# One layer of a gated hybrid block: the second block of x loaded through ScalarE's queue

## The chip, the core and the metric

The kernel runs on one core of a Trainium2 chip. A core has a matrix engine (TensorE, PE in the profile), whose weight loads are listed apart (PEld), and three engines for everything else: VectorE (DVE), ScalarE (ACT) and GpSimd (POOL). SyncE (SP) only issues transfers. ScalarE and GpSimd can issue transfers too. Each issuing engine has a queue of its own; the transfers themselves are carried by the core's 16 DMA engines.

The metric is the device time of one execution in microseconds, the median of several runs.

## What is computed

One layer over a sequence of 512 positions and 1024 channels, all in float32:

```python
h = rms_norm(x, norm_mix_g)
cb, cc, cin, q, k, v, f_logit, g_logit = split(h @ w_in)
y_conv = (cb * causal_dwconv(cc * cin, conv_mix_w)) @ w_out_conv
o = forgetting_attention(q, k, v, log_sigmoid(f_logit + b_f))    # 8 heads of 64, causal
g_conv, g_attn = split(sigmoid(g_logit + b_gate))
x = x + (g_conv * y_conv + g_attn * (o @ w_out_attn)) @ w_o
h = rms_norm(x, norm_ffn_g)
a, b = split(causal_dwconv(h @ w_up, conv_ffn_w))                # 2 x 2816
x = x + (silu(a) * b) @ w_down
out = rms_norm(x, norm_f_g)
```

Only the beginning matters here: the first part of `h @ w_in`, the columns for v and for the forget logits.

## The kernel before

**Layout and precision.** x comes transposed as `xT`, 128 partitions x 8 blocks x 512 positions: block kb holds channels 128 kb to 128 kb + 127. A product in float32 is made of three faster ones: each operand is split into a high part in the reduced type fp32r and a low part, the remainder, and TensorE adds high x high, low x high and high x low in PSUM. For a weight, the high part is a copy (`wh`) and the low part a subtraction (`wl`); for x, the copy is scaled by the norm's gain from the small table `vec` (`xgh`), and the low part is one multiply-and-subtract (`xgl`). The division by the root mean square is put on later, when results leave PSUM.

**Start.** The first work of TensorE is a loop over the eight blocks kb (lines 452 to 500). For each, 24 matmuls multiply x's block with the weight block `v{kb}` (128 x 520 values): 4 tiles of 128 positions, two column groups (`pa` of 264 columns, `pb` of 256), three products each. All eight blocks add up in the same banks of PSUM. Ahead of the loop nine warm-up matmuls on a tile of ones keep TensorE busy (line 115). Block 0 is taken in smaller pieces: its x comes in two halves, and its weights in two parts, which ScalarE's queue (line 179) and SyncE's queue (line 180) issue.

**The preparation of a block.** For blocks 0 and 1, VectorE makes `wh` (lines 271 and 273); from block 2 on, ScalarE (line 275). VectorE makes all `wl` (line 279) and `xgl` (line 467). ScalarE makes `xgh` (line 458), then squares of x for the norm. In block 1 `xgh` is written ahead of the weight's split.

**Loading.** The weights of the whole kernel are one list, `stream`; `load` issues its next entries, at first a few blocks ahead, later as buffers come free. x is loaded by `load_x`. The order at the start is this:

```python
load_x(0, halves[0])
load(0)
load_x(0, halves[1])
for kb in range(1, AHEAD + 1):      # AHEAD = 3
    load_x(kb)
    load(kb)
for kb in range(AHEAD + 1, KB):
    load_x(kb)
```

All of `load_x` and all of `load` but the first part of weight block 0 goes through SyncE's queue. `vec` goes through GpSimd's (line 99). On ScalarE a small activation (line 110) stands ahead of line 179; it makes the engine load its function table.

**What sets the order.** Instructions passed to `keep` stay in program order on their engine. These are all matmuls, all transfers of `load` and `load_x`, and the preparation of the eight v blocks. The others are placed by the framework's planner, which also sets which instruction waits for which semaphore; a small list `later` with due positions and time allowances, written by hand, decides where in the program much of the later work is put. Transfers of SyncE and ScalarE take their completion semaphores in turn from a small set, so a transfer can be held until an earlier one has landed.

**After the start.** The projections for attention and convolution (`p_in`, `p_q`, `p_k`), attention, gates, `w_o`, and the channel mixer (`p_up`, `dn`) follow, all driven by the same weight stream. Part of the large products uses seven block products in place of eight; the sums of weight blocks that this needs are formed by adding transfers on GpSimd's queue (line 211). These stages are not touched by the change.

Of the kernel before, what the change touches and what calls it, by code (L numbers as in the profile page):

```python
# [70 lines left out]
def block_kernel(ctx, tc, xT, vecs, wv, win, wmix, wo, wup, wst, wdp, outT):  # L71
# [3 lines left out]
    nc = tc.nc  # L75
# [6 lines left out]
    def keep(ins):  # L82
        return tc.keep_in_program_order(ins)
# [334 lines left out]
    xs = []  # L418

    def load_x(kb, cs=slice(0, S)):  # L420
        if kb == len(xs):
            if kb % 2 == 0:
                if kb == 4:
                    ap.tile([P, S], F32, tag="pp", name="pp_", bufs=NPP)
                    ap.tile([P, 4], F32, tag="m", name="m_", bufs=6)
                load_x.t = ap.tile([P, 2, S], F32, tag="qt" if kb < 4 else "ka", name=f"xs{kb}", bufs=2)
            xs.append(load_x.t[:, kb % 2, :])
        keep(nc.sync.dma_start(xs[kb][:, cs], xT[:, kb, cs]))


    halves = [slice(0, S // 2), slice(S // 2, S)]
# [3 lines that stand above are left out]
    for kb in range(1, AHEAD + 1):  # L435
        load_x(kb)
        load(kb)
# [1100 lines left out]
```

## Time and profile before

| | |
|---|---|
| median of 3 runs | 693.18 us (693.14 to 693.18) |
| the profiled execution | 693.12 us |
| its span in the profile | 691.3 us |
| TensorE busy | 681.8 us, 99% of the span |
| VectorE, ScalarE, GpSimd busy | 80%, 53%, 28% |
| bytes moved by transfers | 137.54 MB |

The span goes from the first to the last instruction of the program; the time of the execution holds 1.8 us more. In the rows of the profile, L428 is line 428 of the kernel. "PEq", "SPq" and so on are the sequencers, which issue and wait. A row of the time line gives start and duration in us, engine, line, operation, what it writes and reads, its shape, how many were merged into it, and in brackets how long the engine had been idle and what ended that. A row of the waits gives who waited for whom, the total in us, how often, and the longest. `raw_v` is the landing place of the v weight blocks, `xs` that of x's blocks.

### The profile page before, as it was taken

To read this page: it belongs to the slowest core of one execution; us is meant where nothing else is said; L and a number is where in the kernel's file an instruction comes from. 1 tells how busy PE (TensorE), PEld (TensorE's weight loads), DVE (VectorE), ACT (ScalarE), POOL (GpSimd) and SP (SyncE) were. 2 spreads that over 40 slices of the span, in tenths; PEclk is the share of its full clock that TensorE was granted. 3 is DMA by queue.
4 is the path that set the end of the run, shared out by engine and by line. 5 is a ranking of instruction groups with operands and counts; after the bars stand their busy time and mean duration, and the time that the engine had idled before them with its cause. 6 is when DMAs were issued, how large, how long until landed. Compare 5 with 4: busy or idle time off the path is not lost.

```text
span 691.3 us, 14713 instructions
## 1 busy us (share of the span) xinstructions
PE 681.8 (99%) x5936; PEld 679.9 (98%) x5936; DVE 555.2 (80%) x861; ACT 367.9 (53%) x581; POOL 192.7 (28%) x203
## 2 busy tenths in 40 slices
PE   8999999999999999999999999999999999999996
PEld 8999999999999999999999999999999999999995
DVE  5777887967578778868879699998787898988894
ACT  5675755555555444446564455546444545445672
POOL 6124947542020201214400144340100314332000
PEclk9999999999999999999999999999999999999998
DMA  8628999562577686788997498888945986876513
GB/s 291 240 62 287 217 246 208 129 134 92 167 162 210 166 261 198 239 310 210 161 315 230 129 251 216 184 233 253 250 148 187 288 256 162 191 167 161 192 31 123
DMA packets 66165, 137.54 MB, mean 199 GB/s; under 512 B 5888, under 2 KB 31760, under 8 KB 65840
## 3 DMA queue, kind: packets, MB, share of 16 engines
q1 hardware_dynamic: 45384, 107.28, 46.9%
q0 software_dynamic: 18896, 26.03, 24.4%
q10 hardware_dynamic: 1816, 3.29, 1.3%
q8 instruction: 46, 0.75, 0.4%
q14 instruction: 23, 0.19, 0.1%
HBM read 132.31 MB, written 47.71 MB: 260 GB/s over the span
## 4 chain that ended last, share of the span: by engine, by line
PE 94%; DVE 3%; DMA 1%; ACT 0%; issue 0%; SPq 0%; DVEq 0%; ACTq 0%
PE dn L327 28%; PE p_up L309 18%; PE p_in L309 14%; PE p_wo L309 6%; PE p_up L327 5%; PE yc L309 3%; PE ya L309 3%; PE p_q L309 2%; PE p_k L309 2%; PE o L658 2%; PE pa L477 2%; PE pb L479 1%; PE tp L641 1%; PE pdB L309 1%; PE pdA L309 1%; DVE wl_up L279 1%
## 5 line engine op out<-in xcount | busy, mean ns | idle before, releaser
L211 POOL DMA_DIRECT2D f<-in_wst_dram x69 | 80.0, 1367 | 26.7 <-DMA f<-f 26.3
L309 PE MATMUL p_up<-x1h,wh_up 128*128 128x256 f32 x416 | 81.1, 276 | 0.0
L309 PE MATMUL p_up<-x1h,wl_up 128*128 128x256 f32 x416 | 81.0, 276 | 0.0
L309 PE MATMUL p_up<-x1l,wh_up 128*128 128x256 f32 x416 | 81.0, 276 | 0.0
L279 DVE TENSOR_TENSOR wl_F<-raw_F,wh_F 128x1024 fp32r<-128x1024 f32 (+1 forms) x43 | 56.1, 1304 | 19.0 <-ACT wh_F L275 18.9
L275 ACT ACTIVATE wh_F<-raw_F 128x1024 fp32r<-128x1024 f32 (+1 forms) x43 | 44.5, 1035 | 40.8 <-PE dn L327 26.4
L309 PEld LDWEIGHTS p_up<-x1h,wh_up 128*128 128x128 f32 x416 | 62.7, 188 | 0.0
L309 PEld LDWEIGHTS p_up<-x1l,wh_up 128*128 128x128 f32 x416 | 62.6, 188 | 0.0
L309 PEld LDWEIGHTS p_up<-x1h,wl_up 128*128 128x128 f32 x416 | 62.6, 188 | 0.0
L1234 POOL TENSOR_TENSOR ge<-fu,fu 128x512 f32<-128x512 f32 x11 | 23.2, 2108 | 123.3 <-DVE fu L570 92.6
L309 PE MATMUL p_in<-xgh,wh_in 128*128 128x256 f32 x288 | 56.8, 279 | 0.0
L309 PE MATMUL p_in<-xgh,wl_in 128*128 128x256 f32 x288 | 56.6, 278 | 0.0
L309 PE MATMUL p_in<-xgl,wh_in 128*128 128x256 f32 x288 | 56.5, 278 | 0.0
L275 ACT ACTIVATE wh_P<-raw_P 128x768 fp32r<-128x768 f32 (+1 forms) x43 | 35.2, 820 | 34.5 <-PE dn L327 23.1
L279 DVE TENSOR_TENSOR wl_P<-raw_P,wh_P 128x768 fp32r<-128x768 f32 (+1 forms) x43 | 41.7, 970 | 14.6 <-ACT wh_P L275 8.6
L279 DVE TENSOR_TENSOR wl_up<-raw_up,wh_up 128x1024 fp32r<-128x1024 f32 x34 | 45.2, 1328 | 7.5 <-ACT wh_up L275 7.4
L327 PE MATMUL dn<-gh,wh_F 128*128 128x256 f32 x216 | 51.0, 276 | 0.0
L327 PE MATMUL dn<-gl,wh_F 128*128 128x256 f32 x216 | 51.0, 276 | 0.0
L275 ACT ACTIVATE wh_up<-raw_up 128x1024 fp32r<-128x1024 f32 x34 | 35.8, 1054 | 20.4 <-PE p_up L309 9.8
L309 PEld LDWEIGHTS p_in<-xgh,wh_in 128*128 128x128 f32 x288 | 44.7, 188 | 0.7
L309 PEld LDWEIGHTS p_in<-xgl,wh_in 128*128 128x128 f32 x288 | 43.7, 188 | 0.0
L309 PEld LDWEIGHTS p_in<-xgh,wl_in 128*128 128x128 f32 x288 | 43.6, 188 | 0.0
(343 smaller groups left out, 2208.5 us busy)
## 6 DMA issues: line engine op xcount, KB each, us to landing
raw_F<-f SPq DMA_DIRECT2D x40, 512.0 KB, 5.8
raw_up<-in_wup_dram SPq DMA_DIRECT2D x34, 512.0 KB, 5.6
raw_P<-in_wst_dram SPq DMA_DIRECT2D x40, 384.0 KB, 5.9
raw_in<-in_win_dram SPq DMA_DIRECT2D x24, 512.0 KB, 4.1
f<-in_wst_dram POOLq DMA_DIRECT2D x41, 256.0 KB, 7.7
f<-in_wst_dram SPq DMA_DIRECT2D x19, 512.0 KB, 7.1
f<-in_wst_dram POOLq DMA_DIRECT2D x19, 512.0 KB, 8.4
f<-f SPq DMA_DIRECT2D x38, 256.0 KB, 6.0
```

The source lines that it names most:

```text
L211: return lambda: keep(nc.gpsimd.dma_start(dst, src, accum_op=ALU.add))
L275: ins = nc.scalar.activation(hi, raw, AF.Copy)
L279: ins = nc.vector.tensor_sub(lo, raw, hi.bitcast(F32))
L309: keep(nc.tensor.matmul(out[:, cs], w, x[:, cs], start=start and i == 0 and c == 0, stop=stop and i == 2 and c == len(cut) - 1,))
L327: keep(nc.tensor.matmul(out, wl if x == 1 else wh, xl if x == 2 else xh, start=opens and bk not in seen, stop=closes and bk not in left,))
L477: keep(nc.tensor.matmul(pa[t][:, :VW], xt, w[:, VB:], start=start, stop=stop))
L479: keep(nc.tensor.matmul(pb[t], xt, w[:, :VB], start=start and t % 2 == 0, stop=stop and t % 2 == 1))
L641: keep(nc.tensor.transpose(tp[:, ks], pt[:, ks], ident))
L658: keep(nc.tensor.matmul(o[:, 2 * P * e + c0 : 2 * P * (e + 1)], w, x[:, kb, c0:], start=e == 0 and kb == 0 and i == 0, stop=e == 1 and kb ...
L1234: keep(nc.gpsimd.tensor_mul(ge, a.rearrange(halves_of, h=2), b.rearrange(halves_of, h=2)))
```

## The change

The transfer of block 1 of x is issued by ScalarE in place of SyncE. All other blocks stay with SyncE, and the place of the call in the program stays the same.

```diff
@@ -425,7 +425,7 @@
                     ap.tile([P, 4], F32, tag="m", name="m_", bufs=6)
                 load_x.t = ap.tile([P, 2, S], F32, tag="qt" if kb < 4 else "ka", name=f"xs{kb}", bufs=2)
             xs.append(load_x.t[:, kb % 2, :])
-        keep(nc.sync.dma_start(xs[kb][:, cs], xT[:, kb, cs]))
+        keep((nc.scalar if kb == 1 else nc.sync).dma_start(xs[kb][:, cs], xT[:, kb, cs]))
```

## The prediction, made before the result was known

> **What bounds the kernel now.** I read the page first, then the waits of TensorE, then the busy time by stage. From the page:
>
> ```profile
> span 691.3 us, 14713 instructions
> ...
> PE 94%; DVE 3%; DMA 1%; ACT 0%; issue 0%; SPq 0%; DVEq 0%; ACTq 0%
> ```
>
> The chain that ended last is matmuls for 94% of the span; transfers are 1% of it. The waits of TensorE, all that there are, and the busy time by stage (columns of the second: stage, its length, busy us of each engine, granted clock, DMA share, GB/s) say where the other part lies:
>
> ```profile
> PE warm L115 <- DVE ones L107: 1.1, 1, 1.1
> PE pa L477 <- DVE wh_v L273: 0.8, 1, 0.8
> PE p_up L327 <- DVE wl_up L279: 0.7, 1, 0.7
> ...
> 0.00:8.80 8.80, 6.79 (x42) 6.43 (x43) 3.41 (x8) 3.64 (x6) 7.29 (x21) 1.00 0.71 218
> 8.80:30.00 21.20, 21.20 (x178) 21.20 (x179) 15.07 (x23) 12.12 (x20) 5.37 (x9) 1.00 0.87 313
> 30.00:660.00 630.00, 629.22 (x5506) 628.00 (x5506) 515.44 (x792) 338.63 (x530) 180.00 (x175) 1.00 0.75 201
> ```
>
> From 8.80 us on TensorE has no idle time until 30, and 0.78 us in the 630 us after that. So whatever moves the matmul at 8.80 moves the end by as much, if the rest is left in its order; and TensorE's whole idle time from its first real matmul to 660 us is 0.8 + 0.7 us. That caps a gain at the start at 0.84 us, the idle time just before 8.80. The chain of waits over the first 60 us says what ends that idle time:
>
> ```profile
> 1.65 0.43 SPq L428
> 2.12 0.43 SPq L428
> 2.60 5.46 DMA raw_v<-in_wv_dram
> 8.09 0.58 DVE wh_v L273
> ...
> 8.80 0.36 PE pa L477
> ```
>
> It runs back from the matmul to VectorE's copy of weight block 1 (v1 below), to the 5.46 us from that transfer's issue to its landing, and then to SyncE's own issue instructions. The issue at 2.12 is the one that the change takes away from SyncE: the second block of x (x1). It stands on the chain, directly ahead of v1.
>
> **The change part by part.** It removes one issue from SyncE's queue, adds one to ScalarE's, and puts x1's 256 KB behind ScalarE's own first transfer in place of behind x0's second half. The queues of SyncE and ScalarE, in order of time (start, us, what):
>
> ```profile
> 1.19 0.42 SPq L180 DMA_DIRECT2D raw_v<-in_wv_dram  x1
> 1.65 0.91 SPq L428 DMA_DIRECT2D xs<-in_xT_dram  x2
> 2.60 0.43 SPq L182 DMA_DIRECT2D raw_v<-in_wv_dram  x1
> 4.97 3.71 SPq L428 DMA_DIRECT2D xs<-in_xT_dram  x4
> ...
> 0.74 1.28 ACT L110 ACT_TABLE_LOAD   x1 [0.74 <-PEq L1524]
> 1.04 0.44 ACTq L179 DMA_DIRECT2D raw_v<-in_wv_dram  x1
> 4.28 0.91 ACT L458 ACTIVATE xgh<-xs,vec 128x256 fp32r<-128x256 f32 x2 [2.04 <-DMA vec<-in_vecs_dram]
> 7.41 0.72 ACT L458 ACTIVATE xgh<-xs,vec 128x512 fp32r<-128x512 f32 x1 [2.22 <-DMA xs<-in_xT_dram]
> 10.06 0.71 ACT L458 ACTIVATE xgh<-xs,vec 128x512 fp32r<-128x512 f32 x1
> ```
>
> *SyncE, removed.* One issue and the step to the next: 2.60 - 2.12 = 0.48 us. v1 is issued at 2.12 instead of 2.60, and each later one up to the first held one 0.48 us earlier. The hold is inside the 3.71 us of four issues near 5 us, which wait for earlier landings. Those are blocks 4 to 7; the DMA queue is full then and TensorE has no gap, so an earlier or later release there costs nothing.
>
> *ScalarE, added.* One issue of 0.44 us (the price of its row at 1.04), right behind that row: about 1.5 to 1.95. It is covered: ScalarE does nothing after its table work until 4.28, 2.04 us idle, waiting for the small table vec. Without that cover it would cost 0.44. SyncE's 0.42 at 1.19 overlaps ScalarE's 0.44 at 1.04, and neither is longer than the others, so two queues issuing side by side cost nothing extra here. x1 itself is issued about 0.6 us earlier than at 2.12.
>
> *When v1 lands.* The last landing in the chain is v1's, at 2.60 + 5.46 = 8.06. If its time in flight stays 5.46, it lands 0.48 earlier: copy at 7.61, matmul at 8.32. That is the first term: 0.48 us. It is bounded below by nothing gained, since the same engines must move the same bytes ahead of v1 (x0, v0, x1). It is bounded above by the other thing that the matmul group needs, its predecessor.
>
> *The group before.* The 24 matmuls of block 0:
>
> ```profile
> 4.84 0.51 PE L477 MATMUL pa<-wh_v,xgh 128*128 128x264 f32 x2
> ...
> 7.57 0.39 PE L479 MATMUL pb<-wh_v,xgl 128*128 128x256 f32 x2
> ```
>
> They end at 7.96, so the idle time is 8.80 - 7.96 = 0.84, and restart cannot be earlier than 7.96. This group may itself come later: x1 now runs beside v0 and x0's second half instead of behind them. What x1 can take from them depends on the rate (by stage, the busy time of the instructions on x alone, then granted clock, DMA share, GB/s):
>
> ```profile
> 2.00:4.00 2.00, 0.00 (x0) 0.00 (x0) 1.00 0.97 275
> 4.00:6.00 2.00, 0.65 (x2) 0.91 (x2) 1.00 0.69 166
> 6.00:8.00 2.00, 0.22 (x1) 0.59 (x1) 1.00 0.98 349
> 10.00:24.00 14.00, 3.79 (x6) 7.24 (x13) 1.00 1.02 372
> ```
>
> At 372 GB/s, 262,144 bytes are 0.70 us. So block 0 ends between 7.96 (x1 stays behind) and 8.66 (all of x1 goes ahead of what block 0 needs). With half of x1 ahead, the middle, it is 8.31: no later than v1's own 8.32. I take restart at 8.33, a gain of 0.47, with 0 and 0.84 as ends.
>
> *What is late next.* Block 2's group starts 24 matmuls after 8.80, about 11.65, and at 11.18 in the forecast. Its x is ready at 10.06 + 0.71 = 10.77 even if it does not move at all. So block 2 does not give the gain back, and its weights were issued earlier too.
>
> **The sum.** Span 691.3 - 0.47 = 690.83. The profiled execution took 693.12, 1.82 more than its span and 0.06 less than the median of 693.18; 690.83 + 1.82 + 0.06 = 692.71, taken as 692.7, 0.07% under the time before. That is less than the 0.2% (1.39 us) which a measurement of this kernel can tell from no change. The likeliest case's own range is 692.3 (the whole 0.84) to 693.2.
>
> **The rivals.**
>
> *Hidden: the engines share.* x1 takes its turn beside v0 and x0, so block 0 ends later by what v1 gains. Speaking for it: DMA share is 0.97 from 2 to 4 us, when x1 would start. Against it: from 4 to 6 us the share is 0.69 at 166 GB/s, so there is room that x1 and v1 could use. With all 0.70 us ahead of block 0 the restart is at 8.66, a gain of 0.14: 693.0; if v1 also lands as before, 693.2. [...]
>
> *Slower: x1's slow start stands ahead of block 0.* One row speaks for it: x1 landed only at 7.41, while x0's second half was in use by 4.28 + 0.91 - 0.49 = 4.70, with the shortest of these activations here:
>
> ```profile
> L458 ACT ACTIVATE xgh<-xs,vec x9: 493/709/724, 4.3 to 24.0; 128x512 fp32r<-128x512 f32 x7, 128x256 fp32r<-128x256 f32 x2
> ```
>
> So 256 KB took up to 2.71 us, where 0.70 would do: the 166 GB/s stretch. If that slowness belongs to x1's reads and now holds the engines while v0, vec and x0's second half are queued, block 0 ends at 7.96 + 2.71 = 10.67, 1.87 us after 8.80: 695.05. It decides from a delay of block 0 over 0.84 us on; over 2.23 us it is slower by more than 0.2%. Against it: x0 and v0 are issued earlier than x1 on both queues.
>
> *The planner orders the rest anew.* Only what stands under `keep` has a written order; the others are placed by the framework's planner, which sees another start. What one such order costs, from the 0.7 us wait above (ScalarE's row, then VectorE's):
>
> ```profile
> 605.68 1.05 ACT L275 ACTIVATE wh_up<-raw_up 128x1024 fp32r<-128x1024 f32 x1
> ...
> 606.22 1.80 DVE L1261 TENSOR_TENSOR gl<-go,gh 128x512 fp32r<-128x512 f32 x2
> 607.95 0.74 DVE L567 SCALAR_TENSOR_TENSOR fu<-fz,vec,fu 128x511 f32<-128x511 f32 x1
> 608.61 1.21 DVE L279 TENSOR_TENSOR wl_up<-raw_up,wh_up 128x1024 fp32r<-128x1024 f32 x1
> ```
>
> wh_up is done at 606.73, but wl_up stands behind three others and starts at 608.61, and TensorE idles 0.73. Two more such places give 694.2 beside the forecast's gain, four 695.6, and four without that gain 696.1. One fewer gives at best 693.18 - 0.84 - 0.73 = 691.6. There is little left to win by order and much to lose. Against it: past block 0 all work hangs on TensorE's pace, so a shift alike for all engines leaves the order as it is.
>
> **How the numbers follow.** Forecast (restart between 7.96 and 8.70, order kept) 0.43. Hidden (693.0 to 693.2) 0.20. Slow start ahead of block 0 0.12, of which 0.07 over 0.2%. New order 0.25: 0.20 over 0.2% slower, 0.03 faster by more, 0.02 within. Faster: 0.04 and 0.01 for a gain that adds up from both, 0.05; slower 0.07 + 0.20 = 0.27; within 0.2%: 0.68. The range goes from 692.3 (whole idle time gone) to 696.1 (four such waits more); it leaves out about 0.06 below and 0.12 above.
>
> **What would show it.** Right: x1's issue on ScalarE's queue near 1.5; v1's issue at about 2.1; VectorE's copy of v1 near 7.6; block 1's first matmul near 8.33; and TensorE's waits after that the same two in number, the late one about 0.47 us earlier. Hidden: the first matmuls of block 0 after 4.84 stretched, block 1 at 8.66 or later. Slow start: waits of ScalarE or VectorE for x or weights inside block 0. New order: a longer list of TensorE's waits past 30 us. The prediction is wrong if block 1 starts after 8.80, or if new waits past 30 us add up to more than 0.5 us.

## The result and the profile after

The changed kernel is slower: 695.80 us median of 7 runs (693.86 to 696.64) against 693.14 for the kernel before (692.77 to 693.41). The ratio, estimated from all these runs, is 1.0033, with a 95% interval from 1.0023 to 1.0043. The forecast was 692.7. The profiled execution took 694.50 us, one of the quicker ones of the changed kernel; its span is 692.7.

The page, and the waits of TensorE, of the changed kernel:

```profile
span 692.7 us, 14713 instructions
...
PE 94%; DVE 3%; DMA 1%; ACT 0%; issue 0%; DVEq 0%; ACTq 0%; POOLq 0%
```

```profile
PE pa L477 <- ACT xgh L458: 1.4, 1, 1.4
PE warm L115 <- DVE ones L107: 1.1, 1, 1.1
PE p_up L327 <- DVE wl_up L279: 0.7, 1, 0.7
```

The list is as short as before, and the late wait is the same, so nothing past the start was ordered anew. The wait for VectorE's copy of weight block 1 is gone, since block 0 now ends later than that copy. A wait for `xgh`, the scaled copy of x's block 0, stands in its place, and it is longer: 1.4 us where 0.8 was. The chain of waits over the first 12 us says why (start, us, what):

```profile
1.28 4.77 DMA vec<-in_vecs_dram
6.07 0.52 ACT xgh L458
6.63 0.51 PE pa L477 x2
```

The chain no longer runs through v1 but through `vec`, the table of 20 KB that GpSimd's queue brings. It is issued at 1.28 as before, but takes 4.77 us where ScalarE's wait for it ended at 4.28 before. ScalarE's and SyncE's queues, VectorE's `xgl` of block 0 and its copy of v1, and TensorE where block 0 ends and block 1 begins, all of the changed kernel:

```profile
1.04 0.43 ACTq L179 DMA_DIRECT2D raw_v<-in_wv_dram  x1
1.51 0.45 ACTq L428 DMA_DIRECT2D xs<-in_xT_dram  x1
...
6.07 1.71 ACT L458 ACTIVATE xgh<-xs,vec 128x256 fp32r<-128x256 f32 x3 [3.84 <-DMA vec<-in_vecs_dram]
```

```profile
1.65 0.43 SPq L428 DMA_DIRECT2D xs<-in_xT_dram  x1
2.12 0.43 SPq L182 DMA_DIRECT2D raw_v<-in_wv_dram  x1
```

```profile
6.61 1.07 DVE L467 SCALAR_TENSOR_TENSOR xgl<-xs,vec,xgh 128x256 fp32r<-128x256 f32 x2 [1.19 <-ACT xgh L458]
7.60 0.46 DVE L273 CAST wh_v<-raw_v 128x520 fp32r<-128x520 f32 x1
```

```profile
9.49 0.40 PE L479 MATMUL pb<-wh_v,xgl 128*128 128x256 f32 x2
9.72 0.28 PE L477 MATMUL pa<-wh_v,xgh 128*128 128x264 f32 x1
```

v1 was issued at 2.12, as forecast, and its copy began at 7.60, half a microsecond earlier. That 7.60 is not v1's landing: VectorE came to the copy straight from `xgl` of block 0, which the late vec had held up. The earlier copy did not help: block 0 started at 6.63 instead of 4.84, and block 1 followed it without a gap at 9.72 instead of 8.80. The 1.79 us are 0.84 of idle time used up and 0.92 lost, within 0.03. Note the issue times: x1 at 1.51 on ScalarE's queue, x0's second half at 1.65 on SyncE's. The change put x1 ahead of a transfer that block 0 needs.

Who had the DMA engines from 2 to 4 us, by queue (packets, MB, share of 16 engines; q10 is ScalarE's, q1 SyncE's, q0 GpSimd's), before:

```profile
q1 hardware_dynamic: 423, 0.39, 66.9%
q10 hardware_dynamic: 144, 0.14, 26.4%
q0 software_dynamic: 32, 0.02, 3.4%
```

and after:

```profile
q10 hardware_dynamic: 214, 0.27, 53.4%
q1 hardware_dynamic: 271, 0.24, 38.5%
q0 software_dynamic: 8, 0.01, 1.5%
```

Before, all 32 packets of `vec` were through by 4 us; after, 8 of them were. ScalarE's queue doubled its bytes in that stretch, and SyncE's lost 0.15 MB.

This explains +0.92 of the 1.38 us by which the profiled execution is longer. The medians differ by 2.66; most of that further difference is a second mechanism, which this one profile does not hold and the next one does.

### The profile page after: what moved, and what is told of

It reads as the page before. It is cut to its first block, busy times and chain, and to the rows that moved or that the text cites. A ratio compares the mean times of both kernels' runs of the same rounds, so it can differ in the third digit from the quotient of the medians.

```text
span 692.7 us, 14713 instructions
## 1 busy us (share of the span) xinstructions
PE 682.3 (98%) x5936; PEld 680.4 (98%) x5936; DVE 555.1 (80%) x861; ACT 368.1 (53%) x581; POOL 192.4 (28%) x203
## 4 chain that ended last, share of the span: by engine, by line
PE 94%; DVE 3%; DMA 1%; ACT 0%; issue 0%; DVEq 0%; ACTq 0%; POOLq 0%
PE dn L327 28%; PE p_up L309 18%; PE p_in L309 14%; PE p_wo L309 6%; PE p_up L327 5%; PE yc L309 3%; PE ya L309 3%; PE pa L477 2%; PE pb L479 2%; PE p_q L309 2%; PE p_k L309 2%; PE o L658 2%; PE tp L641 1%; PE pdB L309 1%; PE pdA L309 1%; DVE wl_up L279 1%
```

## The experiments

Each ratio is against the kernel before as timed beside that run; its medians there were 692.79 us (a1, vec_act, the two runs on the layout of x), 693.09 (the pace of TensorE, extra, x1_late) and 693.16 (the others).

**The changed kernel again.** No edit.

> The changed kernel once more, unaltered, for a second profile. Theory A (sharing): the packets of the second block of x stand ahead of the small table vec and of x0's second half on the 16 DMA engines, and by how much differs from execution to execution. Then the landing of vec is late again (after 5 us, 4.26 before), ScalarE's first xgh starts at it, block 1's matmuls start after 9 us, and the span grows by about what block 1's start grows; the times scatter over 2 us or more. Theory B (chance): the late vec of the one profile was an outlier and something later in the kernel costs the time; then vec lands near 4.3 here, and the waits of TensorE past 30 us are longer than 0.7 us.

695.59 us (695.17 to 695.87), ratio 1.0036 [1.0024, 1.0048]; its profiled execution, 695.17. TensorE's rows of block 0 and the first of block 1:

```profile
6.25 0.81 PE L477 MATMUL pa<-wh_v,xgh 128*128 128x264 f32 x2 [0.99 <-ACT xgh L458]
6.86 0.63 PE L479 MATMUL pb<-wh_v,xgh 128*128 128x256 f32 x2
...
9.46 0.44 PE L479 MATMUL pb<-wl_v,xgh 128*128 128x256 f32 x2
9.73 0.40 PE L477 MATMUL pa<-wh_v,xgl 128*128 128x264 f32 x2
...
10.68 0.28 PE L477 MATMUL pa<-wh_v,xgh 128*128 128x264 f32 x1
```

The five times lie within 0.7 us, so the scatter of 2 us that theory A expected is not in this set. vec was late again, and a little less so: block 0 starts at 6.25, not 6.63. Yet block 1 starts at 10.68, not 9.72. Two matmuls take 0.63 us here, and 0.40 us from 9.73 on; they begin 0.215 us apart, and then 0.12. TensorE ran at half its pace for the first 14 matmuls of block 0. In the first profile of the change it had its full pace from the first one. So the span grew by 2.1 us here and by 1.4 there, with vec late in both. Sharing explains the late start, but not the difference between the two; theory B fell, since the waits past 30 us are the same. The profile's clock column reads 1.00 in all these stretches and does not show the half pace. The distances between the starts of the matmuls do.

**The pace of TensorE.** The warm-up matmuls (two rows of the trace each) run from 1.05 us to about 5 and keep TensorE busy until block 0. In the kernel before, block 0 follows at once. A late block 0 leaves a gap. Two edits change only the gap, from both sides:

```diff
-NWARM = 9
+NWARM = 13     # on the changed kernel
```

> The changed kernel with 13 warm-up matmuls in place of 9, so that TensorE has no gap of a microsecond between warm-up and block 0. Theory E (two steps: late vec moves block 0 by 1 to 1.8 us, and the gap in TensorE's work that this leaves puts off the grant of the full clock, at random, so that block 0's 24 matmuls go at 0.215 instead of 0.12 us each): the grant comes before 7.5 us in every execution, block 1 starts at 9.5 to 9.9, the time falls from 695.6 to 693.8 to 694.5 and the scatter of 2.8 us (693.86 to 696.64) shrinks under 1 us. Theory F (late transfers alone): nothing changes, 695.6 with the same scatter.

694.17 us (693.62 to 694.80), ratio 1.0017 [1.0008, 1.0025]. vec was late all the same (ScalarE waited for it until 5.86), but the gap is filled:

```profile
5.90 0.75 PE L115 MATMUL warm<-ones 128*128 128x128 f32 x4
6.42 0.51 PE L477 MATMUL pa<-wh_v,xgh 128*128 128x264 f32 x2
6.76 0.39 PE L479 MATMUL pb<-wh_v,xgh 128*128 128x256 f32 x2
```

```diff
-NWARM = 9
+NWARM = 6      # on the kernel before
```

> The kernel before with 6 warm-up matmuls in place of 9: the transfers are untouched, but TensorE now has a gap of about 1.2 us ahead of block 0. Theory E: the full clock is granted after 7 us in many executions, block 0's matmuls go at 0.215 us there, block 1 starts at up to 10, and the median rises by 0.3 to 1.5 us with a scatter over 1.5 us. Theory F: the same time as before, within 0.2 us, since block 0 starts at 4.84 either way.

694.05 us (692.78 to 695.62), ratio 1.0015 [1.0006, 1.0024], with no transfer of block 0 over 0.1 us later (vec was there at 4.35 instead of 4.28):

```profile
4.91 0.81 PE L477 MATMUL pa<-wh_v,xgh 128*128 128x264 f32 x2 [0.93 <-ACT xgh L458]
5.51 0.63 PE L479 MATMUL pb<-wh_v,xgh 128*128 128x256 f32 x2
...
9.46 0.28 PE L477 MATMUL pa<-wh_v,xgh 128*128 128x264 f32 x1
```

Both medians and both paces came out as theory E has them; the scatter with the gap filled is 1.2 us, where under 1 was expected. Filling the gap takes the change's loss from 1.0036 to 1.0017 and its scatter from 2.8 to 1.2 us. Making such a gap in the kernel before costs it 0.15% with no transfer of block 0 late, and gives it a scatter of 2.8 us, against 1.2 for the kernel before timed beside it. About half of what the change costs is thus the late transfers themselves, and about half the pace. With the gap filled, block 1 starts at 9.75, 0.95 us later than before, and the median is 1.08 longer: that is the share of the late transfers.

Where the clock column shows a stretch of half clock (x1_late and before_vec, below), it lasts 3.4 us. A gap of 0.99 us was followed by 14 matmuls at half pace in a1, and one of 1.37 us by none in the first profile of the change, so the same kernel can be quick in one execution and slow in the next. What decides between the two, no view shown here says.

The gap is not the only way to a late full pace. In the kernel before with x laid out by blocks (xb_before, below), block 0 follows the warm-up directly, and its first 8 matmuls still go at half pace (its first pair of matmuls, and the fifth pair, at full pace):

```profile
4.98 0.81 PE L477 MATMUL pa<-wh_v,xgh 128*128 128x264 f32 x2
6.86 0.41 PE L477 MATMUL pa<-wl_v,xgh 128*128 128x264 f32 x2
```

So the moment of the full pace moves from execution to execution. In the kernel before it came inside the warm-up: its rows begin 0.21 us apart up to 3.99 us and 0.11 from 4.12 on. In xb_before it came by 6.86. Behind a gap it came at about 8.3 in before_w6, 9.5 in a1 and 10.6 in xb_after (below), though by 6.63 in the first profile of the change. The kernel before has long executions too: beside a1, four of its 29 took 694.07 to 696.53 us. Whether the pace made those long, no profile shows.

**Who goes ahead of whom.** First, the transfer added without taking x1 from SyncE:

```diff
     load(0)
+    keep(nc.scalar.dma_start(xt[:, 1, :], xT[:, 1, :]))    # on the kernel before
     load_x(0, halves[1])
```

> The kernel before, all of x's first-stage blocks on SyncE's queue, with one more transfer of 256 KB on ScalarE's queue at the place where the change puts x1 (block 1 of x into the tile xt, which a later transfer of GpSimd fills anyway). Theory A (what the change costs is 256 KB on a second queue at that time, whatever they are): vec lands after 5 us and x0's second half after 5.5, the time is 694.5 to 696.5, at least as slow as the change, since x1 is now moved twice. Theory G (it is the order of x1, or SyncE's queue without it, that costs): vec lands near 4.3 as before and the time stays under 693.6.

695.38 us (693.36 to 699.45), ratio 1.0031 [1.0018, 1.0044]. ScalarE's rows:

```profile
5.72 0.51 ACT L459 ACTIVATE xgh<-xs,vec 128x256 fp32r<-128x256 f32 x1 [3.49 <-DMA vec<-in_vecs_dram]
6.59 0.51 ACT L459 ACTIVATE xgh<-xs,vec 128x256 fp32r<-128x256 f32 x1 [0.36 <-DMA xs<-in_xT_dram]
```

256 KB at that place on a second queue hold up vec to 5.7 us, and x0's second half to 6.6, though nobody waits for them. They read the same part of x as x1 does, so a transfer from elsewhere is not tested. Theory A stands and G falls. The saving on SyncE's queue, which this kernel lacks, is not to be seen in the time.

Second, x1 on ScalarE's queue behind block 0's copies, where nothing that block 0 needs is outstanding:

```diff
         if kb != 1:
             x_hi()
+        if kb == 0:
+            load_x(1, late=True)    # ScalarE issues x1 here, not ahead of the loop
```

> The changed kernel with x1's issue moved on ScalarE's queue behind block 0's two xgh, so that it starts at about 4.6 us, when vec and x0 have landed. Theory A: vec lands by 4.3 and x0's second half by 4.5 as before, v1 lands near 6.5 since x1 no longer stands ahead of it on SyncE's queue, x1 lands between 6.5 and 7.5; block 1 starts at 8.0 to 8.5 and the time is 692.2 to 692.7, under that of before. Theory D: x1, with later blocks of SyncE's queue in flight beside it, lands after 8 and block 1 starts after 9: 693.3 or more.

697.83 us (697.50 to 699.57), ratio 1.0077 [1.0064, 1.0089]: the slowest of all. Theory A's numbers for x1 and for the time were missed; theory D's (x1 after 8 us, 693.3 or more) held. ScalarE's rows, and then who moved packets from 4.4 to 7.5 us and from 7.5 to 9.5:

```profile
4.18 0.51 ACT L459 ACTIVATE xgh<-xs,vec 128x256 fp32r<-128x256 f32 x1 [1.96 <-DMA vec<-in_vecs_dram]
4.40 0.39 ACTq L429 DMA_DIRECT2D xs<-in_xT_dram  x1
...
11.06 0.72 ACT L459 ACTIVATE xgh<-xs,vec 128x512 fp32r<-128x512 f32 x1 [5.97 <-DMA xs<-in_xT_dram]
```

```profile
q1 hardware_dynamic: 494, 0.91, 96.4%
```

```profile
q1 hardware_dynamic: 292, 0.54, 69.5%
q10 hardware_dynamic: 131, 0.24, 32.6%
```

vec and x0 were on time again (4.18), which confirms that x1's early issue is what delayed them. But x1, issued at 4.40 with five transfers of SyncE outstanding, moved no packet until 7.5 us and was there at 11.06. TensorE stood for 3.90 us, began block 1 at 11.83, and then ran at half pace: here the clock column shows it, 0.50 from 11.52 to 14.93. A second queue was no way here around what SyncE's queue had been given. From 2 to 4 us of the changed kernel the two queues do mix (53.4% of the engines' time for ScalarE's, 38.5% for SyncE's), but here x1 moved nothing for 3.1 us. Where the waiting transfer stood in that time, these profiles do not show.

Third, x0's second half in x1's place on ScalarE's queue:

```diff
-        keep((nc.scalar if kb == 1 else nc.sync).dma_start(xs[kb][:, cs], xT[:, kb, cs]))
+        keep((nc.scalar if cs.start else nc.sync).dma_start(xs[kb][:, cs], xT[:, kb, cs]))
```

> Instead of x1, the second half of x0 is issued on ScalarE's queue, third in all at about 1.5 us; x1 is then third on SyncE's queue at about 1.65 and v1 fourth at 2.12. The same issue step is saved as by the change, but x0's second half keeps its place ahead of x1. Theory H (what is issued first is moved first, whichever queue it came by): x0's second half lands by 4.5, x1 by about 7, v1 by about 7.6 instead of 8.06; vec, whose packets come after 3.2 us, may again stand behind x1's and land at 4.5 to 6; the time is 692.6 to 694.5, at least 1 us under the change. Theory I (the two queues take turns, packet by packet): the second half of x0 is no better placed than x1 was, vec lands after 5, 695 to 696.

694.08 us (693.38 to 696.12), ratio 1.0018 [1.0009, 1.0028].

```profile
5.03 0.51 ACT L458 ACTIVATE xgh<-xs,vec 128x256 fp32r<-128x256 f32 x1 [2.81 <-DMA vec<-in_vecs_dram]
5.80 1.12 ACT L458 ACTIVATE xgh<-xs,vec 128x256 fp32r<-128x256 f32 x2 [0.26 <-DMA xs<-in_xT_dram]
```

The time is in theory H's range (692.6 to 694.5), and vec was late by less, 5.03, as it allowed. But x0's second half, which it had in by 4.5, was held until 5.80, though now issued 0.14 us ahead of x1. So 0.14 us is no safe lead and the queues mix in part. Neither theory holds alone. The twelve times fall into two groups, seven from 693.38 to 694.09 and five from 695.25 to 696.12. The profile is of the first group, with 4 matmuls at half pace; 14 of them, as in a1, cost 14 x 0.1 = 1.4 us by estimate (from a1's 0.215 and 0.12 us a matmul), so the pace may well be what parts the groups.

**vec out of the way.** vec first on ScalarE's queue, with x1 there (changed kernel) and without (kernel before):

```diff
-    keep(nc.gpsimd.dma_start(vec[:, :CM], vecs[:, :CM]))
+    keep(nc.scalar.dma_start(vec[:, :CM], vecs[:, :CM]))
```

> The changed kernel with the small table vec issued first on ScalarE's queue instead of GpSimd's; x1 follows on the same queue as its third transfer. Theory A1 (vec is what holds block 0): with vec in by about 3.5 us, block 0 starts near 4.9, block 1 at 8.3 to 8.8 and the time is 692.7 to 693.2. Theory A2 (x0's second half is held by x1 as much as vec is; it landed at 6.63 in the profile of the change against 4.47): the first matmuls come near 4.9, those on the second half of positions wait until about 7, block 1 starts near 9.5 and the time stays at 694 to 696. Theory B: unchanged at 695.8.

On the changed kernel 693.64 us (693.25 to 695.76), ratio 1.0007 [0.9995, 1.0020]. With vec early, x0's second half is what holds block 0:

```profile
3.30 0.51 ACT L458 ACTIVATE xgh<-xs,vec 128x256 fp32r<-128x256 f32 x1 [0.62 <-DMA vec<-in_vecs_dram]
5.92 1.12 ACT L458 ACTIVATE xgh<-xs,vec 128x256 fp32r<-128x256 f32 x2 [2.11 <-DMA xs<-in_xT_dram]
```

The mechanism is A2's, but its time of 694 to 696 was too high: block 1 came at 8.96, not 9.5, since the half only held until 5.92. Most of the loss is gone.

> The kernel before with vec issued first on ScalarE's queue instead of GpSimd's, x1 left on SyncE's. Theory H: vec lands near 3.2, the weights' first part about 0.4 us later than before (near 4.1), so block 0 starts at 4.8 to 5.1; x1 and v1 land as before, block 1 starts at 8.7 to 9.0 and the time is 692.8 to 693.4, no change. With x1 on ScalarE's queue the same edit gave 693.64 against 692.79; the difference between the two is then the price of x0's second half behind x1.

On the kernel before 695.89 us (694.87 to 697.06), ratio 1.0035 [1.0022, 1.0049]; 692.8 to 693.4 had been expected. Block 1 started at 8.52, but a new gap came later (rows of GpSimd, SyncE, ScalarE and TensorE):

```profile
8.04 0.74 POOL L750 DMA_DIRECT2D xt<-in_xT_dram  x1
```

```profile
9.36 4.02 SPq L182 DMA_DIRECT2D raw_v<-in_wv_dram  x4
```

```profile
18.40 0.64 ACT L275 ACTIVATE wh_v<-raw_v 128x520 fp32r<-128x520 f32 x1 [4.45 <-DMA raw_v<-in_wv_dram]
```

```profile
19.70 0.59 PE L477 MATMUL pa<-wh_v,xgh 128*128 128x264 f32 x1 [2.35 <-ACT xgh L458]
20.09 0.42 PE L479 MATMUL pb<-wh_v,xgh 128*128 128x256 f32 x1
```

GpSimd, freed of vec, issued the first of the four transfers for `xt` (2 MB in all) at 8.04 instead of 9.54, ahead of SyncE's next weight block at 9.36. From 12 to 15 us GpSimd's queue took 73.5% of the engines' time, where it took 41.1% before. The weight block was there only at 18.4 instead of 15.58, TensorE stood for 2.35 us, and then ran at half pace (0.42 us a matmul where 0.28 is usual; the clock column reads 0.50 from 19.57 to 22.97). It looks like the change's story at another place: a transfer that nobody waits for yet, issued earlier, goes ahead of one that is needed. How far ahead matters: in vec_act GpSimd began at 8.30, but SyncE issued its weight block at 8.54, and no such wait came. So this run does not give the price of x0's second half, as had been meant.

**Is it the layout of x?** For the first stage alone, x is read from a copy laid out block by block, so that a block's rows are not 16 KB apart:

```diff
-        keep(....dma_start(xs[kb][:, cs], xT[:, kb, cs]))
+        keep(....dma_start(xs[kb][:, cs], xB[kb, :, cs]))
```

> The changed kernel with the eight blocks of x for the first stage read from a copy of x that is laid out block by block, so that a block's 128 rows follow each other in memory instead of lying 16 KB apart. Theory C (the slow stretch from 4 to 6 us comes from the rows being 16 KB apart): the stretch is gone, 256 KB take about 0.7 us, vec lands before 4.8, block 1 starts at 8.0 to 8.5, and the time is 692.3 to 692.9. Theory D (any first transfers of this size are slow there, wherever they read): vec lands after 5 us as in the changed kernel, and the time is 694 to 696.

> The kernel before with the same block-by-block copy of x and all of x's blocks on SyncE's queue. Theory C: x1 lands before 6 us instead of 7.38, v1 before 7, block 1 starts at 7.97 to 8.2, and the time is 692.3 to 692.6. Theory D: nothing changes by more than 0.2 us: block 1 at 8.8, 693.1.

With the change 694.25 us (693.03 to 695.78), ratio 1.0019 [1.0010, 1.0028]; without it 693.14 (692.62 to 695.27), ratio 1.0003 [0.9995, 1.0011]. ScalarE's first copies with the change (first two rows) and its copies of x0's halves and x1 without it:

```profile
5.24 0.51 ACT L458 ACTIVATE xgh<-xs,vec 128x256 fp32r<-128x256 f32 x1 [3.01 <-DMA vec<-in_vecs_dram]
5.97 1.12 ACT L458 ACTIVATE xgh<-xs,vec 128x256 fp32r<-128x256 f32 x2 [0.23 <-DMA xs<-in_xB_dram]
```

```profile
4.42 0.51 ACT L458 ACTIVATE xgh<-xs,vec 128x256 fp32r<-128x256 f32 x1 [2.19 <-DMA vec<-in_vecs_dram]
5.11 0.51 ACT L458 ACTIVATE xgh<-xs,vec 128x256 fp32r<-128x256 f32 x1 [0.18 <-DMA xs<-in_xB_dram]
6.58 0.72 ACT L458 ACTIVATE xgh<-xs,vec 128x512 fp32r<-128x512 f32 x1 [0.96 <-DMA xs<-in_xB_dram]
```

x1 came at 6.58 instead of 7.41, and with the change vec came at 5.24 instead of 6.07, so the layout has a part in the slowness of x1's transfer. It is not all of it: x1 still came 1.47 us after x0's second half (5.11), not 0.70. The times of both runs, and block 1 at 8.78 in the second, are those of theory D, but D allowed no such move of x1; theory C missed the times. Pace blurs both. In the second profile the 8 matmuls at half pace cost 8 x 0.1 = 0.8 us by estimate, so block 0 made way only at 8.78, and v1's copy, which began at 7.40 instead of 8.09, gained nothing. In the first one 22 of block 0's 24 matmuls went at half pace, and its 695.78 us is the longest of the twelve. What the layout is worth at full pace is not shown.

**The saved issue step without the overtaking.** vec first on ScalarE's queue, x0 as one transfer first on SyncE's, with and without the copy of x by blocks:

```diff
-    load_x(0, halves[0])
+    load_x(0)
     load(0)
-    load_x(0, halves[1])
```

> vec first on ScalarE's queue, and x0 as one transfer of 256 KB, first on SyncE's queue: SyncE saves the same 0.48 us issue step ahead of x1 and v1, with no transfer of x1 going ahead of anything that block 0 needs. Theory H: x0 lands at 3.3 to 3.8, block 0 starts near 4.9, v1 lands near 7.6, block 1 starts at 8.0 to 8.4: 692.3 to 692.8, under the time before by the 0.4 us that the change was meant to bring. If the slow stretch of the first transfers with rows of 2 KB now falls on x0, x0 lands after 5 us, block 0 starts after 5.5 with a gap after the warm-up: 693.5 to 695.5.

> The same with the block-by-block copy of x. Theory C, weakened by the two runs with that copy (x1 landed 0.7 to 0.8 us earlier with it, but vec was still late beside it): x0 and x1 each land some tenths earlier than in the run without the copy, and the time is 0 to 0.4 us lower. If the slow stretch falls on whatever comes first, the two are alike within 0.2 us.

693.73 us (693.34 to 694.51), ratio 1.0008 [0.9999, 1.0016], and with the copy 693.19 (692.70 to 694.01), ratio 1.0000 [0.9991, 1.0008]. Theory H's 692.3 to 692.8 was missed; the first time lies in the range of the other reading (693.5 to 695.5), though x0 was in use at 4.39, not after 5. The copy brought 0.54 us, more than theory C's 0 to 0.4. In the first one TensorE waits for VectorE's copy of v0 in front of block 0:

```profile
5.65 0.48 PE L476 MATMUL pa<-wh_v,xgh 128*128 128x264 f32 x2 [0.39 <-DVE wh_v L271]
```

In the second, block 1 starts at 8.53, 0.27 us earlier than before, and short waits behind it, one of them in front of a matmul at 17.56, give that back. No gain of the kind that the change was after is to be seen here, and no kernel of this study beats the kernel before clearly.

## Why the prediction was wrong

*What bounds the kernel.* Right. In the first profile block 1's start moved by 0.92 us, and the last group of TensorE by 0.85 (684.17 to 685.02 in the chain). A further 0.5 us of that span lies behind the last VectorE instruction, in the output's transfers; no run was made on it.

*SyncE removed, ScalarE added, v1's landing.* The issues were right to the hundredth: x1 at 1.51, v1 at 2.12. The copy of v1 at 7.60, against 7.61, is chance: VectorE was busy until then, and in a1 the copy began at 7.38, so v1 was there under 5.3 us after its issue, not after 5.46. The 0.48 us of the issue step were right and worth nothing, since block 0 ended later still.

*The group before.* This is the step that failed. It bounded block 0's end between 7.96 and 8.66, letting x1 take 0.70 us, its time at 372 GB/s, and took 8.31. Block 0 made way for block 1 at 9.72 in one profile and at 10.68 in the other. Three things were wrong in it.
- The full rate was no bound. The same prediction quoted the 166 GB/s stretch, and that x1 took up to 2.71 us. It used this only in a rival.
- That rival was argued down with "x0 and v0 are issued earlier than x1 on both queues". The prediction's own numbers say otherwise: x1 at about 1.5, and x0's second half, the first of the two issues merged in SyncE's row of 1.65, after it.
- Outside that rival, vec was treated as the cover of ScalarE's issue ("waiting for the small table vec"), not as a transfer that x1 could delay. It landed at 6.05 instead of 4.26 and was what held block 0; vec_act shows x0's second half close behind it.

*The idle gap.* No term of the sum had it. A gap in front of block 0 was priced at its own length; in four of the profiles here 14 to 22 of block 0's matmuls behind it also went at half pace (0.215 us each in a1, 0.12 at full pace). The longer warm-up shows it to be about half of the loss. The warm-up matmuls of 0.42 us were in the trace before; the clock column's 1.00, which the prediction quotes, does not show their half pace.

*The rivals.* The one that ended slower, with 695.05 and a chance of 0.12, was the right one, and its mark (waits of ScalarE for x or weights inside block 0) nearly so: the wait was for vec. Its price stands for something else than what happened: it had block 0 end at 10.67 by x1's slowness, and the late transfers alone brought 9.72 (9.75 with the gap filled). That a1 comes to 10.68 is chance, for there the half pace made up the rest. The planner, with 0.25, did nothing: all engines' orders past the moved issue are as before. The upper end of the range, 696.1, stood for four of the planner's waits, so it is luck that 695.80 lies under it. "Hidden" was wrong, and its limit of 0.70 us with it. The chances hold a slip of 0.01: the sum for "faster" starts from 0.04, where the planner's part was given as 0.03.

## What to carry to other kernels

Issuing a transfer earlier on a free queue was not free here: it took the DMA engines from what was issued, or got its packets, after it (vec was in use at 6.07 us instead of 4.28, x0's second half at 6.66 instead of 4.70). List everything outstanding at that moment with its deadline, the small transfers of GpSimd's queue first, and price the moved transfer by the time it takes at that place (up to 2.71 us for x1 in the kernel before), not by the full rate (0.70 us at 372 GB/s). Where TensorE has just been warmed up, price a gap by the pace that it costs as well as by its length (an estimated 1.4 us beside 0.99 in a1), and look at several executions before trusting one profile.

## What the runs showed of the hardware that was not expected

- A gap between warm-up and work (idle 0.99 us in a1, 1.37 in the first profile of the change) left 14 matmuls at 0.215 us each in one execution and none in the other. Without a gap it was none in the kernel before and 8 in xb_before. Behind a gap of 2.35 us later on (before_vec), and behind one of 3.90 us (x1_late), the clock column reads 0.50 for 3.4 us.
- A transfer issued on ScalarE's queue at 4.40 us, behind five of SyncE's, moved no packet until 7.5 us, while a transfer on the same queue issued at 1.51 delayed one of SyncE's issued at 1.65 (x0's second half, in use at 6.66 instead of 4.70).
- x1's 256 KB were in use 2.71 us after x0's second half in the kernel before, and 1.47 us after it with x laid out by blocks; at the 372 GB/s of later blocks they need 0.70. What the rest is stays open.
